# Pooling after the product by banded matrices, GpSimd freed of products in the front, 44 transposed expert tiles prepared ahead on GpSimd's queue

## The chip, the cores and the metric

One core of a Trainium2 chip runs the whole program in one launch. The metric is the device time of one execution, in microseconds (us). Engines are named as in the profile: PE is TensorE, DVE is VectorE, ACT is ScalarE, POOL is GpSimd, SP is SyncE, which issues most of the DMAs.

## The reference, cut to what matters

The input is 512 tokens of 1024 numbers. Two blocks follow each other. The first one is a pooling mixer: `h = x @ w_in`, whose first 2048 columns are `u` (four groups of 512) and the others `z`. For group g with window w in (2, 4, 8, 16):

```python
csum = jnp.cumsum(u, axis=1)
lag = jnp.pad(c, ((0, 0), (w, 0), (0, 0)))[:, :S]
cnt = jnp.minimum(t + 1, w)
outs.append((c - lag) / cnt - u[:, :, g])     # mean of the last w tokens, less the token
m = einsum('bsgc,gcd->bsgd', m, w_grp) * scale
return (m * jax.nn.silu(z)) @ w_out           # then layer_norm(alpha * x + y)
```

The second block computes six modulation vectors `ada = silu(c) @ w_ada + b_ada`, then a gated convolution and a linear recurrence on `h @ w_in`, a head-wise norm and `@ w_out`. After a second norm comes a product-key expert layer: each token chooses 16 of 16384 experts in each of 8 heads, and each chosen expert adds `gate * gelu(h . U[e]) * V[e]`. A last norm ends the program.

## The kernel before, in words

All large products are made in split precision. A weight tile `wraw` is loaded by SP (`wload`, line 124), ACT rounds it to `whi` (L113), and DVE (L117) or POOL (L115) subtracts to get the rest `wlo`. `mm3` (L139 to L141) then makes three PE products for one: high by high, high by low, low by high. A counter, `nload`, deals the subtractions out between DVE and POOL, with the constant `NZ` and the line `nload[1] = 3` setting how many POOL gets.

**The front** (0 to about 355 us in the profile) handles the four pooling groups. `z_group` makes the gate columns, `x_group` makes the windowed sums of x itself on DVE (doubling steps `sw`, L240, then `xe`, L244 to L247, and its split `al`), before any product. It works from `xT`, which POOL builds by four additions at L210. `m_group` multiplies the pooled input with w_in, `gate_group` with w_grp, `y_group` with w_out. The last group, `last_group`, does the latter two in halves. Beside them run the modulation vectors: `ada` loads pieces of w_ada (`araw`) and adds them up on DVE (`acc`, L341, L343), and `ada_fin` splits one sum (`ahl`: ACT, then POOL), reduces it over the partitions by two PE products (L352, L353), adds the bias (L354) and stores 512 numbers to `ada_d` (L355). The table `AF_` says where in a group's turn the four `ada_fin` of the group before are called. The pieces `ahl` share four buffers with `araw`.

**The middle** (371 to about 700 us) has the convolution and recurrence in chunks, the product with w_out, the second norm, the queries and the scores. In this stretch `pre_u` turns 20 tiles of U (128 experts each) round ahead of time: for each half tile four loads `praw` of 64 KB (L535), one DVE transpose to `put` (L540), and a store to the DRAM tile `ut_d`. All loads and stores go through SP's queue.

**The gate tables** (700 to 955 us) are made by one-hot products (L1133, L1135, L1136), and beside them the first expert tiles are worked on by `stage_a`, which makes `U tile @ h`. Here U tiles come in three ways, by tile number i: below `NU` a load of the prepared `ut` from `ut_d`; from there up to tile 37 a load of the raw rows turned by PE (L882, with ACT L884 and DVE L886 behind it); in the last loop a raw load `uraw` and a DVE transpose of the whole tile (L540).

**The last loop** (about 1055 to 1900 us) works through the other expert tiles: `stage_a`, the gates, and the product with V. Beside it POOL issues 256 indirect DMAs (L1181, `gu` and `gv`) for one block of tokens, whose products DVE makes (L1193, L1204).

A scheduler orders the instructions of each engine ahead of time from estimated costs; on the chip each engine and each queue then runs its own list strictly in order, waiting on semaphores.

Of the kernel before, what the change touches and what calls it, by code (L numbers as in the profile page):

```python
# [7 lines left out]
F32 = mybir.dt.float32  # L8
# [36 lines left out]
GP0 = 4  # L45
GL = 1
GE = 117
NU = 20
PU = (1,)
CB = 13  # L50
PL = 0
# [6 lines left out]
UB = 2  # L58
NQ = 3
LAG = 1  # L60
NUR = 3
NP = (0, 1)
HP = ()
WQ = 1
# [15 lines left out]
def _body(tc, nc, a, outer):  # L80
# [51 lines left out]
    def wcols(w, c0, n):  # L132
        return wload(w[:, c0:c0 + n].rearrange("(k p) c -> p k c", p=P), KD)
# [39 lines left out]
    sp_ = p1.enter_context(tc.tile_pool(name="sp_", bufs=3))  # L173
    adp = p1.enter_context(tc.tile_pool(name="adp", bufs=1))
    xT = xp.tile([P, KD, T], F32, name="xT")

    def act_tiles():
        return ([act.tile([P, 2, T], F32R, name="ah", tag="ah") for _ in range(4)],
# [2 lines left out]
    def at(pair, k):  # L181
        return pair[0][k // 2][:, k % 2, :], pair[1][k // 2][:, k % 2, :]
# [32 lines left out]
    def cv(name, i=0, n=1):  # L215
        return cols[:, col[name][0] + i:col[name][0] + i + n]

    def z_group(g, other=()):
        r = []
        for c in range(4):  # L220
            next(iter(other), None)
            if b_first:
                b = b_first.pop(0)
            else:
                w = wcols(w_in, 2048 + (g * 4 + c) * P, P)
                b = bank()
                for k in range(KD):
                    mm3(b, (w[0][:, k], w[1][:, k]), at(xhl, k), k == 0, k == KD - 1)
            r.append(sm.tile([P, T], F32, name="sz", tag="sz", bufs=5))
            S.activation(r[c], b, AF.Silu)  # L230
        return r

    def x_group(g, xg):
        w_ = WINDOWS[g]
        for q in range(4):
            src = xT[:, 2 * q:2 * q + 2, :]
            cur, step = src, 1
            while step < w_:
                nxt = sp_.tile([P, 2, T], F32, name="sw", tag="sw")
                V.tensor_tensor(nxt[:, :, step:], cur[:, :, step:], cur[:, :, :T - step], op=OP.add)  # L240
                S.activation(nxt[:, :, :step], cur[:, :, :step], AF.Copy)
                cur, step = nxt, 2 * step
            e = sp_.tile([P, 2, T], F32, name="xe", tag="sw")
            V.scalar_tensor_tensor(e, cur, 1.0 / w_, src, op0=OP.mult, op1=OP.subtract)  # L244
            n = w_ - 1
            V.tensor_tensor(e[:, :, :n], cur[:, :, :n], rcnt[:, None, :n].to_broadcast([P, 2, n]), op=OP.mult)
            V.tensor_tensor(e[:, :, :n], e[:, :, :n], src[:, :, :n], op=OP.subtract)  # L247
            split(xg[0][q], xg[1][q], e)
            yield

    def m_group(g, xg):
        r = []
        for c in range(4):
            w = wcols(w_in, g * 512 + c * P, P)
            b = bank()
            for k in range(KD):
                mm3(b, (w[0][:, k], w[1][:, k]), at(xg, k), k == 0, k == KD - 1)
            h = sm.tile([P, T], F32R, name="sh", tag="sh")
            l = sm.tile([P, T], F32R, name="sl", tag="sl")
            split(h, l, b)  # L260
            r.append((h, l))
        return r

# [108 lines left out]
    b = bank()  # L372
# [155 lines left out]
    U, W = a["expert_u_2"][0], a["expert_v_2"][0]  # L528
    ut_d = tc.dram_tile([max(1, NU), P, 2, KD * 64], F32, name="ut_d")
    npre = 0  # L530

    def u_load(raw, i, a0, na):

        for q in (0, 2, 1, 3):
            nc.sync.dma_start(raw[32 * q:32 * q + 32],  # L535
                              U[i * P + a0 * 32:i * P + (a0 + na) * 32, q * 256:(q + 1) * 256].rearrange("(a r) d -> r a d", r=32))

    def u_turn(ut, raw):

        V.transpose(out=ut.rearrange("p k (a r) -> p a k r", r=32), in_=raw.rearrange("p a (c k) -> p a k c", k=KD))  # L540

    def pre_u(n):

        nonlocal npre
        for _ in range(n):
            if npre < NU:
                for h in range(2):
                    raw = up.tile([P, 2, 256], F32, name="praw", tag="praw")
                    u_load(raw, npre, 2 * h, 2)
                    ut = up.tile([P, KD, 64], F32, name="put", tag="put")  # L550
                    u_turn(ut, raw)
                    nc.sync.dma_start(ut_d[npre, :, h], ut.rearrange("p k e -> p (k e)"))
                npre += 1
# [664 lines left out]
    urp = outer.enter_context(tc.tile_pool(name="urp", bufs=NUR, reuse_waits="tile"))  # L1218
# [77 lines left out]
```

## Time and profile before

| | |
|---|---|
| median of 3 runs | 1996.67 us (1991.03 to 1996.69) |
| profiled execution | 1993.15 us, its span 1991.4 us |
| mean granted PE clock | 0.968 of full speed |
| busy share of the span | PE 90%, DVE 90%, ACT 42%, POOL 37% |
| chain that ended last | DVE 36%, DMA 24%, PE 17%, issue 12%, ACT 7% |

Between the profiled execution's time and its span lie 1.75 us. The busy shares are means over stages with different limits, so the views by stretch of time say more than this table: in one stretch PE may be full and DVE loose, in the next the other way round.

### The profile page before, as it was taken

To read this page: it belongs to the slowest core of one execution; us is meant where nothing else is said; L and a number is where in the kernel's file an instruction comes from. 1 tells how busy PE (TensorE), PEld (TensorE's weight loads), DVE (VectorE), ACT (ScalarE), POOL (GpSimd) and SP (SyncE) were. 2 spreads that over 40 slices of the span, in tenths; PEclk is the share of its full clock that TensorE was granted. 3 is DMA by queue.
4 is the path that set the end of the run, shared out by engine and by line. 5 is a ranking of instruction groups with operands and counts; after the bars stand their busy time and mean duration, and the time that the engine had idled before them with its cause. 6 is when DMAs were issued, how large, how long until landed. Compare 5 with 4: busy or idle time off the path is not lost.

```text
span 1991.4 us, 26565 instructions
## 1 busy us (share of the span) xinstructions
PE 1800.5 (90%) x9003; PEld 1568.3 (79%) x9003; DVE 1783.6 (90%) x3088; ACT 830.8 (42%) x1318; POOL 727.5 (37%) x492
## 2 busy tenths in 40 slices
PE   8999889896899978888887999998999998989997
PEld 6787677765689978888766898888888887878886
DVE  8989888889868999996897998999999999999956
ACT  4433333444553339988332332333232333332334
POOL 3113222333351000000133655556565556565514
PEclk9999999998899989999998999999999999999999
DMA  5554574465554233545959999999999999999922
GB/s 163 180 166 128 190 250 131 140 203 179 172 159 135 76 112 139 202 179 205 294 199 281 299 285 292 302 296 309 306 298 296 310 299 289 305 293 306 293 102 96
DMA packets 288293, 441.13 MB, mean 222 GB/s; under 512 B 24600, under 2 KB 203652, under 8 KB 285084
## 3 DMA queue, kind: packets, MB, share of 16 engines
q1 hardware_dynamic: 251292, 305.19, 51.1%
q0 software_dynamic: 36864, 134.23, 20.5%
q8 instruction: 71, 1.16, 0.2%
q14 instruction: 66, 0.54, 0.1%
HBM read 393.11 MB, written 46.23 MB: 221 GB/s over the span
## 4 chain that ended last, share of the span: by engine, by line
DVE 36%; DMA 24%; PE 17%; issue 12%; ACT 7%; SPq 2%; POOL 2%; DVEq 0%; POOLq 0%; ACTq 0%
DMA uraw<-in_expert_u 11%; DVE ut L540 5%; DMA gu<-in_expert_u,idx 3%; DMA gv<-in_expert_v,idx 3%; DMA araw<-in_w_ada 3%; PE bank L139 3%; PE bank L141 3%; PE bank L140 3%; ACT gs L1136 2%; DVE acc L1204 2%; DVE ul L117 2%; DVE wlo L117 2%; ACT o L1098 2%; DVE junk L1193 2%; DVE sw L240 2%
## 5 line engine op out<-in xcount | busy, mean ns | idle before, releaser
L115 POOL TENSOR_TENSOR wlo<-wraw,whi 128x1024 fp32r<-128x1024 f32 x111 | 292.3, 2635 | 782.4 <-ACT whi L113 766.8
L141 PE MATMUL aux<-h2h,ul 128*128 128x384 f32 x1024 | 360.7, 353 | 59.8 <-DVE ul L117 53.5
L139 PE MATMUL aux<-h2h,uh 128*128 128x384 f32 x1024 | 355.9, 348 | 4.9 <-ACT uh L884 1.8
L140 PE MATMUL aux<-h2l,uh 128*128 128x384 f32 x1024 | 353.6, 345 | 0.0
L113 ACT ACTIVATE whi<-wraw 128x1024 fp32r<-128x1024 f32 x218 | 228.3, 1051 | 196.4 <-DMA wraw<-in_expert_v 68.5
L140 PE MATMUL o<-wlo,wh 128*128 128x512 f32 x756 | 297.7, 394 | 13.8 <-DVE wlo L117 13.7
L141 PE MATMUL o<-whi,wl 128*128 128x512 f32 x756 | 296.6, 392 | 0.0
L139 PE MATMUL o<-whi,wh 128*128 128x512 f32 x756 | 290.1, 395 | 5.2 <-ACT whi L113 5.2
L141 PEld LDWEIGHTS aux<-h2h,ul 128*128 128x128 f32 x1024 | 198.6, 194 | 76.6 <-DVE ul L117 68.7
L1181 POOL DMA_INDIRECT gv<-in_expert_v,idx x128 | 186.8, 1460 | 186.0 <-DVE acc L1204 150.4
L1181 POOL DMA_INDIRECT gu<-in_expert_u,idx x128 | 167.5, 1309 | 161.3 <-DVE junk L1193 127.7
L139 PEld LDWEIGHTS aux<-h2h,uh 128*128 128x128 f32 x1024 | 198.6, 194 | 10.3 <-ACT gl L905 2.4
L113 ACT ACTIVATE uh<-ut 128x1024 fp32r<-128x1024 f32 x90 | 95.3, 1058 | 262.2 <-PE aux L140 174.5
L540 DVE STREAM_TRANSPOSE ut<-uraw 128x1024 f32<-128x1024 f32 x90 | 200.0, 2222 | 4.7 <-DMA uraw<-in_expert_u 4.7
L140 PEld LDWEIGHTS aux<-h2l,uh 128*128 128x128 f32 x1024 | 197.9, 193 | 3.7
L1193 DVE SCALAR_TENSOR_TENSOR junk<-gu,hrow 128x1024 bf16<-128x1024 f32 x128 | 168.3, 1315 | 19.8 <-DMA gu<-in_expert_u,idx 19.6
L1204 DVE SCALAR_TENSOR_TENSOR acc<-gv,cf,acc 128x1024 f32<-128x1024 f32 x127 | 169.6, 1335 | 17.6 <-DMA gv<-in_expert_v,idx 15.1
L140 PEld LDWEIGHTS o<-wlo,wh 128*128 128x128 f32 x756 | 143.3, 190 | 43.9 <-DVE wlo L117 16.5
L113 ACT ACTIVATE wh<-gl 128x384 fp32r<-128x384 f32 x128 | 66.7, 523 | 253.2 <-PE o L140 234.3
L139 PEld LDWEIGHTS o<-whi,wh 128*128 128x128 f32 x756 | 143.3, 190 | 33.0 <-ACT whi L113 6.1
L141 PEld LDWEIGHTS o<-whi,wl 128*128 128x128 f32 x756 | 143.3, 189 | 30.7
L117 DVE TENSOR_TENSOR wlo<-wraw,whi 128x1024 fp32r<-128x1024 f32 x107 | 150.6, 1409 | 7.2 <-ACT whi L113 7.2
(376 smaller groups left out, 3607.4 us busy)
## 6 DMA issues: line engine op xcount, KB each, us to landing
wraw<-in_expert_v SPq DMA_DIRECT2D x128, 512.0 KB
uraw<-in_expert_u SPq DMA_DIRECT2D x360, 128.0 KB
araw<-in_w_ada SPq DMA_DIRECT2D x96, 256.0 KB
g_d<-gs SPq DMA_DIRECT2D x24, 1024.0 KB
gt<-g_d SPq DMA_DIRECT2D x15, 1536.0 KB
wraw<-in_pool_w_in SPq DMA_DIRECT2D x32, 512.0 KB
wraw<-in_w_in SPq DMA_DIRECT2D x20, 512.0 KB
praw<-in_expert_u SPq DMA_DIRECT2D x160, 64.0 KB
```

Source lines behind the costliest of these rows:

```text
L113: S.activation(hi, src, AF.Copy)
L115: G.tensor_tensor(lo, src, hi.bitcast(F32), op=OP.subtract)
L117: V.tensor_tensor(lo, src, hi.bitcast(F32), op=OP.subtract)
L139: i = PE.matmul(out, lhsT=l[0], rhs=r[0], start=first, stop=False)
L140: PE.matmul(out, lhsT=l[0], rhs=r[1], start=False, stop=False)
L141: PE.matmul(out, lhsT=l[1], rhs=r[0], start=False, stop=last)
L240: V.tensor_tensor(nxt[:, :, step:], cur[:, :, step:], cur[:, :, :T - step], op=OP.add)
L540: V.transpose(out=ut.rearrange("p k (a r) -> p a k r", r=32), in_=raw.rearrange("p a (c k) -> p a k c", k=KD))
L1098: S.activation(o2[:, u], iorow, AF.Abs, bias=sT[:, 1, t0 + u:t0 + u + 1], scale=-1.0)
L1181: G.indirect_dma_start(out=r, out_offset=None, in_=src, in_offset=bass.IndirectOffsetOnAxis(ap=idx[t][:, s:s + 1], axis=0))
L1193: paced(V.scalar_tensor_tensor(junk, r, 1.0, hrow[t], op0=OP.mult, op1=OP.mult, accum_out=cf[t][:, s:s + 1]))
L1204: paced(V.scalar_tensor_tensor(acc[t], r, cf[t][:, s:s + 1], acc[t], op0=OP.mult, op1=OP.add))
```

## The change

1. `u_group` multiplies x with w_in first (x stationary, as many products of 512 columns as `m_group` had), and `pooled` then makes the windowed mean by products with banded 128x144 matrices. In each group these are 32 products of 128 columns and 28 of 16 columns, so 240 in all. `bands` builds the matrices once, with some 40 small DVE instructions. `x_group`, `xT` and the split `al` of the pooled input go; the u columns are split instead (16 ACT, 16 DVE, straight from PSUM). The weights of u come as 2 KB pieces instead of 512 B ones.
2. `NZ` and `nload` leave POOL no product in the front and the middle: POOL's `wlo` go from 111 to 63, DVE's from 107 to 155. The 12 `ahl` go from POOL to DVE.
3. `NU` is 44 instead of 20, and `pre_u` starts in the front: 24 tiles (48 half tiles) there, 20 later. Its loads and stores are issued from POOL's queue (`G`), five DMAs per half tile. In `stage_a` the 18 tiles that PE turned and the first six of the last loop become loads from `ut_d`.
4. `AF_` moves the last four `ada_fin` behind the last `y_group`.

```diff
-AF_ = (1, 1, 0, 0)
-NZ = 1
+AF_ = (1, 1, 1)
+NZ = 1 << 30
-NU = 20
+NU = 44
+NP1 = 1
-    for q in range(4):
-        G.tensor_tensor(xT[:, 2 * q:2 * q + 2, :], xh[:, q].bitcast(F32), xl[:, q].bitcast(F32), op=OP.add)
-    def x_group(g, xg):
...
-    def m_group(g, xg):
...
+    def u_group(g):
+        bs = [bank() for _ in range(NT)]
+        for kk in range(4):
+            w = wload(w_in[kk * 256:(kk + 1) * 256, g * 512:(g + 1) * 512].rearrange("(k p) c -> p k c", p=P), 2)
+            for t in range(NT):
+                s = slice(t * P, (t + 1) * P)
+                for j in range(2):
+                    x = at(xhl, 2 * kk + j)
+                    mm3(bs[t], (x[0][:, s], x[1][:, s]), (w[0][:, j], w[1][:, j]), kk + j == 0, kk == 3 and j == 1)
...
+        for t in range(NT):
+            split(uh[t // 2][:, t % 2], ul[t // 2][:, t % 2], bs[t])
+    def pooled(g, u):
...
+        for c in range(4):
+            b = bank()
+            part = lambda t, i: u[i][t // 2][:, t % 2, c * P:(c + 1) * P]
+            for t in range(NT):
+                m = (band if t else first)[:, :P]
+                o = b[:, t * P:(t + 1) * P]
+                e = o[:, :16]
+                PE.matmul(o, lhsT=part(t, 0), rhs=m, start=True, stop=False)
+                if t == 0:
+                    PE.matmul(e, lhsT=part(t, 0), rhs=rest, start=False, stop=False)
+                else:
+                    PE.matmul(e, lhsT=part(t - 1, 0), rhs=band[:, P:], start=False, stop=False)
+                    PE.matmul(e, lhsT=part(t - 1, 1), rhs=band[:, P:], start=False, stop=False)
+                PE.matmul(o, lhsT=part(t, 1), rhs=m, start=False, stop=True)
...
-        split(hi, lo, acc, True)
+        split(hi, lo, acc)
+                    u_load(raw, npre, 2 * h, 2, G)
...
+                    G.dma_start(ut_d[npre, :, h], ut.rearrange("p k e -> p (k e)"))
-    nload[1] = 3
-    for g in range(4):
-        mhl = m_group(g, xg)
...
+    mhl = pooled(0, u)
+    for g in range(3):
+        pre_u(NP1)
+        u = u_group(g + 1)
+        pre_u(NP1)
+        pre_u(NP1)
         ghl = gate_group(g, mhl, sz)
         if AF_[g] == 1:
             ada_fins()
+        sz = z_group(g + 1)
+        pre_u(NP1)
+        mhl = pooled(g + 1, u)
...
         for _ in y_group(g, ghl):
-            pass
+            pre_u(1)
+    ada_fins()
```

The order of the instructions shows three places, the last of them on two engines. On DVE, at the head of the front (splits of the transposed x, `xl`, then those of the first u weights), the changed program has half-tile transposes between the splits that PE waits for:

```order
L203 TENSOR_TENSOR xl_124<-bank_192,xh_123 128x4x128
L118 TENSOR_TENSOR wlo_242<-wraw_239,whi_241 128x1024
L407 STREAM_TRANSPOSE put_635<-praw_630 128x2x8x32
L203 TENSOR_TENSOR xl_124<-bank_199,xh_123 128x4x128
L407 STREAM_TRANSPOSE put_643<-praw_638 128x2x8x32
L118 TENSOR_TENSOR wlo_272<-wraw_269,whi_271 128x1024
L118 TENSOR_TENSOR wlo_302<-wraw_299,whi_301 128x1024
L407 STREAM_TRANSPOSE put_787<-praw_782 128x2x8x32
L118 TENSOR_TENSOR wlo_332<-wraw_329,whi_331 128x1024
L407 STREAM_TRANSPOSE put_795<-praw_790 128x2x8x32
L118 TENSOR_TENSOR wlo_376<-wraw_373,whi_375 128x1024
```

Before, no transpose stood on DVE ahead of the middle; now each stands in front of a `wlo`, which cannot start until the transpose has its `praw`.

On POOL, in the same place, the list before had the additions to `xT` and the subtractions:

```order
L210 TENSOR_TENSOR xT<-xh,xl 128x1024 x4
L115 TENSOR_TENSOR wlo<-wraw,whi 128x1024 x6
L115 TENSOR_TENSOR ahl<-acc,ahl 128x512
L115 TENSOR_TENSOR wlo<-wraw,whi 128x1024 x2
L115 TENSOR_TENSOR ahl<-acc,ahl 128x512 x3
```

and now has the traffic of the half tiles alone:

```order
L419 DMA ut_d_234<-put_635 128x512
L402 DMA praw_782<-in_expert_u_2 32x2x256 x4
L419 DMA ut_d_234<-put_643 128x512
L402 DMA praw_790<-in_expert_u_2 32x2x256 x4
L419 DMA ut_d_234<-put_787 128x512
```

A store, which waits for its transpose, stands ahead of the four loads of the half tile two further on.

On SP, on the way into `last_group`, whose weights are `pool_w_grp` and the `pool_w_out` behind it, the list before was

```order
L339 DMA araw<-in_w_ada 128x512 x4
L124 DMA wraw<-in_pool_w_grp 128x4x256 x2
L339 DMA araw<-in_w_ada 128x512 x3
L124 DMA wraw<-in_pool_w_in 128x8x128
L339 DMA araw<-in_w_ada 128x512 x2
L124 DMA wraw<-in_pool_w_out 128x2x512 x2
```

and now is

```order
L373 DMA araw<-in_w_ada 128x512 x28
L382 DMA araw<-in_b_ada 1x512 x2
L472 DMA lng<-in_ln_g 128x1024
L472 DMA lnb<-in_ln_b 128x1024
L472 DMA g1r<-ada_d 128x1024
L389 DMA ada_d<-araw 1x512
L382 DMA araw<-in_b_ada 1x512
L389 DMA ada_d<-araw 1x512
L382 DMA araw<-in_b_ada 1x512
L541 DMA acol<-ada_d 128x2x8
L389 DMA ada_d<-araw 1x512 x2
```

followed by loads of `n2` and of `vin2` (the latter from `ada_d`) and only then by the two loads of `pool_w_grp`. So these weights stand behind the four stores that end the `ada_fin`. On PE the same place reads now

```order
L141 MATMUL bank_3076<-wlo_2983,sh_2530 128x512
L142 MATMUL bank_3076<-whi_2982,sl_2531 128x512
L386 MATMUL aux_3108<-ahl_3109,ones_88 1x512
L387 MATMUL aux_3108<-ahl_3110,ones_88 1x512
L386 MATMUL aux_3119<-ahl_3120,ones_88 1x512
L387 MATMUL aux_3119<-ahl_3121,ones_88 1x512
L386 MATMUL aux_3130<-ahl_3131,ones_88 1x512
L387 MATMUL aux_3130<-ahl_3132,ones_88 1x512
L386 MATMUL aux_3141<-ahl_3142,ones_88 1x512
L387 MATMUL aux_3141<-ahl_3143,ones_88 1x512
L571 MATMUL aux_3416<-ident_84,vin2_3174 128x128
L140 MATMUL bank_3236<-sh_2742,whi_3194 128x256
```

with the last product of `y_group` (bank_3076) and the first of `last_group` (bank_3236) on either side of all four `ada_fin` and of a transpose that reads `vin2`, loaded from `ada_d`. Before, the `ada_fin` pairs stood between products of `m_group` and `last_group`.

## Rows read from the trace of the kernel before

**Rows 1.** The page: busy time of the engines; the chain that ended last.

```profile
PE 1800.5 (90%) x9003; PEld 1568.3 (79%) x9003; DVE 1783.6 (90%) x3088; ACT 830.8 (42%) x1318; POOL 727.5 (37%) x492
...
DVE 36%; DMA 24%; PE 17%; issue 12%; ACT 7%; SPq 2%; POOL 2%; DVEq 0%; POOLq 0%; ACTq 0%
```

**Rows 2.** Busy us by stretch, front: PE, PEld, DVE, ACT, POOL, clock, DMA, GB/s.

```profile
100.00:150.00 50.00, 50.00 (x217) 40.32 (x216) 44.97 (x61) 15.42 (x24) 9.04 (x4) 1.00 0.53 162
...
sum 350.00, PE 324.36 PEld 260.99 DVE 315.66 ACT 128.25 POOL 94.06; mean PE 46.34 PEld 37.28 DVE 45.09 ACT 18.32 POOL 13.44
```

**Rows 3.** Groups by line, 0 to 350 us: operation, count, busy us, mean ns, idle, releasers.

```profile
L343 DVE SCALAR_TENSOR_TENSOR acc<-araw,cact,acc 128x512 f32<-128x512 f32 x84 | 70.8, 844 | 14.4 <-DMA araw<-in_w_ada 13.3 <-DVE acc L343 0.3
...
L117 DVE TENSOR_TENSOR wlo<-wraw,whi 128x1024 fp32r<-128x1024 f32 x39 | 55.7, 1430 | 1.9 <-ACT whi L113 1.9
L115 POOL TENSOR_TENSOR wlo<-wraw,whi 128x1024 fp32r<-128x1024 f32 x19 | 54.9, 2892 | 178.9 <-ACT whi L113 178.8
...
L240 DVE TENSOR_TENSOR sw<-xT 128x1022 f32<-128x1022 f32 x16 | 23.8, 1487 | 0.0
...
L117 DVE TENSOR_TENSOR al<-xe,ah 128x1024 fp32r<-128x1024 f32 x16 | 22.7, 1423 | 0.4 <-ACT ah L113 0.4
...
L117 DVE TENSOR_TENSOR sl<-bank,sh 128x512 fp32r<-128x512 f32 x16 | 10.8, 681 | 4.3 <-ACT sh L113 4.3
```

**Rows 4.** Groups by line, 700 to 955 us, the gate tables.

```profile
L1135 PE MATMUL bank<-og,o 128*128 128x128 f32 x768 | 99.6, 283 | 20.5 <-ACT gs L1136 10.5 <-ACT o L1099 9.8 <-DVE og L1133 0.2
...
L1136 ACT ACTIVATE gs<-bank 128x512 f32<-128x512 f32 x96 | 93.7, 1088 | 0.4 <-DMA g_d<-gs 0.3
...
L882 PE MATMUL aux<-ident,uraw 128*128 128x128 f32 x144 | 21.5, 276 | 2.9 <-ACT gl L905 2.9
L884 ACT ACTIVATE uh<-aux 128x512 fp32r<-128x512 f32 x35 | 20.8, 611 | 5.1 <-PE aux L882 5.1
```

**Rows 5.** Tile ahl, 310 to 345 us: ns min/median/max, first and last start us.

```profile
L113 ACT ACTIVATE ahl<-acc x4: 622/632/632, 316.3 to 329.4; 128x512 fp32r<-128x512 f32 x4
L115 POOL TENSOR_TENSOR ahl<-acc,ahl x4: 1287/1786/2060, 317.7 to 330.7; 128x512 fp32r<-128x512 f32 x4
...
L352 PE MATMUL aux<-ahl,ones x4: 393/396/397, 318.0 to 334.3; 128*1 128x512 f32 x4
```

**Rows 6.** Groups by line, 371 to 600 us, the middle.

```profile
L115 POOL TENSOR_TENSOR wlo<-wraw,whi 128x1024 fp32r<-128x1024 f32 x27 | 67.3, 2494 | 121.2 <-ACT whi L113 109.3 <-DMA praw<-in_expert_u 11.9
...
L540 DVE STREAM_TRANSPOSE put<-praw 128x512 f32<-128x512 f32 x40 | 46.2, 1158 | 12.8 <-DMA praw<-in_expert_u 12.7
...
L620 PE MATMUL aux<-sq,blk 128*128 128x512 f32 x16 | 13.2, 932 | 27.4 <-ACT sq L616 27.4
```

**Rows 7.** Busy us by stretch, the last loop.

```profile
1100.00:1900.00 800.00, 746.33 (x3626) 667.37 (x3625) 760.86 (x767) 254.06 (x356) 458.65 (x291) 0.98 1.01 298
```

**Rows 8.** Groups by line, 1100 to 1900 us, the last loop.

```profile
L540 DVE STREAM_TRANSPOSE ut<-uraw 128x1024 f32<-128x1024 f32 x85 | 189.3, 2227 | 0.0
L1181 POOL DMA_INDIRECT gv<-in_expert_v,idx x128 | 186.8, 1460 | 186.0 <-DVE acc L1204 150.4 <-DMA uraw<-in_expert_u 12.4 <-issue 6.4
...
L1181 POOL DMA_INDIRECT gu<-in_expert_u,idx x119 | 157.7, 1325 | 139.9 <-DVE junk L1193 112.6 <-DMA uraw<-in_expert_u 9.2 <-issue 8.1
...
L113 ACT ACTIVATE uh<-ut 128x1024 fp32r<-128x1024 f32 x86 | 91.0, 1058 | 241.8 <-PE aux L140 174.5 <-DVE ut L540 42.4 <-issue 17.0
```

**Rows 9.** The chain, 1050 to 1085 us: start us, us, what.

```profile
1056.72 11.19 DMA uraw<-in_expert_u
```

**Rows 10.** Line 1181, all of the run: ns min/median/max.

```profile
L1181 POOL DMA_INDIRECT gv<-in_expert_v,idx x128: 939/1296/3298, 1123.3 to 1881.7; - x128
```

**Rows 11.** POOL's timeline, 1450 to 1458 us: start us, us, what.

```profile
1453.13 3.30 POOL L1181 DMA_INDIRECT gv<-in_expert_v,idx  x1 [2.81 <-DVE acc L1204]
```

**Rows 12.** DVE's timeline beside it.

```profile
1453.26 1.21 DVE L117 TENSOR_TENSOR wlo<-wraw,whi 128x1024 fp32r<-128x1024 f32 x1
1454.39 1.21 DVE L1193 SCALAR_TENSOR_TENSOR junk<-gu,hrow 128x1024 bf16<-128x1024 f32 x1
```

More of the change, by code (lines that the diff above doesn't have):

```diff
@@ L60 @@
 LAG = 1
-NUR = 3
+BW = P + 16
 NP = (0, 1)
@@ L172, in _body @@
     sm = front2.enter_context(tc.tile_pool(name="sm", bufs=8, side="right"))
-    sp_ = p1.enter_context(tc.tile_pool(name="sp_", bufs=3))
+    up = p1.enter_context(tc.tile_pool(name="up1", bufs=2))
     adp = p1.enter_context(tc.tile_pool(name="adp", bufs=1))
-    xT = xp.tile([P, KD, T], F32, name="xT")
     def act_tiles():
@@ L216, in cv, with z_group @@
         return cols[:, col[name][0] + i:col[name][0] + i + n]
-    def z_group(g, other=()):
+    def z_group(g):
         r = []
         for c in range(4):
-            next(iter(other), None)
             if b_first:
@@ L231, in z_group @@
         return r
-    def x_group(g, xg):
[L234 to L244, printed above, removed]
-            n = w_ - 1
[L246 to L249, printed above, removed]
@@ L251, in m_group, with bands @@
-    def m_group(g, xg):
+    def bands():
+        wide = xp.tile([P, BW], F32, name="wide")
+        past = xp.tile([P, BW], F32, name="past")
+        G.iota(wide, pattern=[[1, BW]], base=0, channel_multiplier=-1, allow_small_or_imprecise_dtypes=True)
+        V.tensor_scalar(past, wide, 0.0, None, op0=OP.is_ge)
+        for g, w_ in enumerate(WINDOWS):
+            n = w_ - 1
+            f = xp.tile([P, BW], F32, name="bandf", tag="bandf", bufs=2)
+            V.scalar_tensor_tensor(f, wide, float(w_), past, op0=OP.is_lt, op1=OP.mult)
+            V.scalar_tensor_tensor(f[:, :P], ident, -float(w_), f[:, :P], op0=OP.mult, op1=OP.add)
+            band = xp.tile([P, BW], F32R, name=f"band{g}")
+            V.tensor_copy(band, f)
+            e = xp.tile([P, 16], F32, name="edge", tag="edge", bufs=2)[:, :n]
+            V.scalar_tensor_tensor(e, rcnt[:, :n], float(w_), past[:, :n], op0=OP.mult, op1=OP.mult)
+            V.scalar_tensor_tensor(e, ident[:, :n], -float(w_), e, op0=OP.mult, op1=OP.add)
+            first = xp.tile([P, BW], F32R, name=f"first{g}")
+            V.tensor_copy(first, f)
+            V.tensor_copy(first[:, :n], e)
+            rest = xp.tile([P, 16], F32R, name=f"rest{g}")
+            V.tensor_scalar(rest, ident[:, :16], 0.0, None, op0=OP.mult)
+            V.tensor_tensor(rest[:, :n], e, first[:, :n].bitcast(F32), op=OP.subtract)
+            band_.append((band, first, rest))
@@ new lines, in _body @@
+    band_ = []
+    def u_group(g):
[7 more added lines that the diff above has]
+                    mm3(bs[t], (x[0][:, s], x[1][:, s]), (w[0][:, j], w[1][:, j]), kk + j == 0, kk == 3 and j == 1)
+        uh = [act.tile([P, 2, T], F32R, name="ah", tag="ah") for _ in range(2)]
+        ul = [act.tile([P, 2, T], F32R, name="al", tag="al") for _ in range(2)]
+        for t in range(NT):
+            split(uh[t // 2][:, t % 2], ul[t // 2][:, t % 2], bs[t])
+        return uh, ul
@@ L252, in m_group @@
+    def pooled(g, u):
         r = []
+        band, first, rest = band_[g]
         for c in range(4):
-            w = wcols(w_in, g * 512 + c * P, P)
             b = bank()
-            for k in range(KD):
-                mm3(b, (w[0][:, k], w[1][:, k]), at(xg, k), k == 0, k == KD - 1)
+            part = lambda t, i: u[i][t // 2][:, t % 2, c * P:(c + 1) * P]
[10 more added lines that the diff above has]
+                PE.matmul(o, lhsT=part(t, 1), rhs=m, start=False, stop=True)
@@ L258, in m_group @@
             h = sm.tile([P, T], F32R, name="sh", tag="sh")
             l = sm.tile([P, T], F32R, name="sl", tag="sl")
-            split(h, l, b)
+            S.activation(h, b, AF.Copy, scale=1.0 / WINDOWS[g])
+            V.scalar_tensor_tensor(l, b, 1.0 / WINDOWS[g], h.bitcast(F32), op0=OP.mult, op1=OP.subtract)
             r.append((h, l))
@@ L359, in ada_fins, with u_load, u_turn, pre_u @@
             ada_fin(j, accs.pop(j))
+    U, W = a["expert_u_2"][0], a["expert_v_2"][0]
+    ut_d = tc.dram_tile([max(1, NU), P, 2, KD * 64], F32, name="ut_d")
+    npre = 0
+    def u_load(raw, i, a0, na, q_=nc.sync):
+        for q in (0, 2, 1, 3):
+            q_.dma_start(raw[32 * q:32 * q + 32],
+                              U[i * P + a0 * 32:i * P + (a0 + na) * 32, q * 256:(q + 1) * 256].rearrange("(a r) d -> r a d", r=32))
+    def u_turn(ut, raw):
+        V.transpose(out=ut.rearrange("p k (a r) -> p a k r", r=32), in_=raw.rearrange("p a (c k) -> p a k c", k=KD))
+    def pre_u(n):
+        nonlocal npre
+        for _ in range(n):
+            if npre < NU:
+                for h in range(2):
+                    raw = up.tile([P, 2, 256], F32, name="praw", tag="praw")
+                    u_load(raw, npre, 2 * h, 2, G)
+                    ut = up.tile([P, KD, 64], F32, name="put", tag="put")
+                    u_turn(ut, raw)
+                    G.dma_start(ut_d[npre, :, h], ut.rearrange("p k e -> p (k e)"))
+                npre += 1
+    u = u_group(0)
     sz = z_group(0)
+    bands()
     vin = pers.tile([P, P], F32, name="vin")
@@ L390, in _body @@
             ada_fins()
-        xg = act_tiles()
-        sz = z_group(g + 1, x_group(g + 1, xg))
+        sz = z_group(g + 1)
+        pre_u(NP1)
+        mhl = pooled(g + 1, u)
         if AF_[g] == 2:
@@ L527, in _body @@
     up = p2.enter_context(tc.tile_pool(name="up", bufs=2, reuse_waits="tile"))
[L528 to L553, printed above, removed]
     lam = cv("lru_lambda_2", 0, 4)
@@ L1217, in _body @@
     banks(outer, AUX)
-    urp = outer.enter_context(tc.tile_pool(name="urp", bufs=NUR, reuse_waits="tile"))
+    urp = outer.enter_context(tc.tile_pool(name="urp", bufs=3, reuse_waits="tile"))
     for i in range(P):
```

6 lines of the change are left out of this document (removed).

## The prediction

> **What bounds the kernel now.** I read the page first [rows 1]: PE and DVE are both busy for 90% of the span, and the chain that ended last spends 36% on DVE, 24% on DMA and only 17% on PE. The mean hides stages with different limits, so the views by stretch come next, then the groups by line within a stretch. The sum is made against the profiled execution, 1993.15 us, which lies 3.5 us below the median of 1996.67.
>
> In the front PE is nearly full: 50.00 us of 50 in one stretch, 324.36 of 350 over all [rows 2]. The same row has DVE busy for 315.66. So PE leads, DVE follows a step behind, and at most 350 - 324.36 = 25.6 us of waiting can be won there. DVE's busy time is inflated: the split `wlo` takes 1430 ns on the mean [rows 3], and 1.21 us where POOL computes nothing beside it [rows 12]. In the middle, PE's large wait is at L620, the head norm, 27.4 us, and it waits there for ACT, whose input comes from DVE [rows 6]. In the gate tables PE stands behind ACT: 10.5 and 9.8 us of its idle time end with ACT instructions [rows 4]. In the last loop DVE is busy 760.86 us of 800 and the DMA engines are full (1.01, 298 GB/s) [rows 7].
>
> **The change part by part.**
>
> *Small products on PE, front.* `u_group` does the work that `m_group` did. New are 128 products of 128 columns and 112 of 16. The trace has no banded product of this type. The nearest row is L1135: 768 products of 128 columns with as many weight loads are busy for 99.6 us, 0.130 us each [rows 4]. 128 x 0.130 = 16.6. The 16 columns cost between nothing and the same 0.130; half of it gives 112 x 0.065 = 7.3. Together **+24**. Lower end: a quarter of a 512-column product (50.00 / 217 = 0.230 us [rows 2]) for the first kind, nothing for the second, 128 x 0.058 = +7. Upper end: each as dear as a 512-column one, 240 x 0.230 = +55. PE is full there, so all of it lies on the path.
>
> *DVE in the front.* Gone are 40 window sums at about 1.49 us (59), the 16 `al` (22.7) [rows 3] and the 16 `xe` of the same size, as much again, 105 in all, and small edge pieces. New are 48 half-tile transposes at 1158 ns (55.6) [rows 6], POOL's 19 `wlo` [rows 3] at 1.21 (23), 28 splits of 512 columns at 681 ns (19), 98 in all, and some 40 small ones for the bands. So the work is equal. What falls is the holding: 39 x (1.43 - 1.21) = 8.6 us on `wlo` alone, and the same on other splits. PE waits less; between nothing and all 25.6. I take **-18**, nearer the upper end, since the two-input DVE instructions show the holding in most of their rows.
>
> *The last four `ada_fin`.* They ran beside other products. Now PE meets all four, then a transpose that reads their result, and `last_group`'s weights stand behind their stores on SP, as the order shows. Before, the first product of the four and the last lie 334.3 - 318.0 = 16.3 us apart, 5.4 each [rows 5]: the pieces share four buffers, so one waits for the store of another. With DVE's 681 ns in place of POOL's 1786 the step is 4.3, four steps 17. Waiting behind them: the weight load, its rounding and split, some 4 us as an estimate from 512 KB at 298 GB/s [rows 7] and 1.2 for DVE. `y_group`'s last adds overlap the first step. **+16**, from 0 (all four end beside `y_group`) to +24.
>
> *The middle.* 27 `wlo` go from POOL (2494 ns) [rows 6] to DVE, 27 x 1.21 = 33 us more there; the DVE instructions that POOL's held up get back about as much. The transposes stay 40. SP loses 200 DMAs that stood ahead of weight loads. **-5**, from -27 (the whole wait at L620) to +24 (POOL too slow, below).
>
> *The gate tables.* 18 tiles give up 36 ACT instructions of 611 ns [rows 4] for 18 of 1058 [rows 8]: 22 - 19 = **-3**. PE's 144 transposes (21.5 us) [rows 4] go too, but lie beside ACT, which had 0.4 us idle before L1136. From -21 to 0.
>
> *The last loop.* Six tiles lose their DVE transpose: 6 x 2.227 [rows 8] = 13.4. Part of the opening wait for raw tiles, 11.19 us in one piece [rows 9], may go with it, since the prepared tiles need no turning; part may stay, since the DMA engines are full. **-14**, from -25 (both) to -2.
>
> *POOL's queue.* 240 DMAs in the front, 200 in the middle. At the shortest issue, 939 ns [rows 10], that is 226 and 188 us, less than the stretches they lie in (about 320 and 229), so **0**. At the mean it is more: first rival.
>
> Sum: 24 - 18 + 16 - 5 - 3 - 14 = 0, so **1993**. Its own range is 1975 to 2012.
>
> **The rivals.**
>
> *POOL's issues are too slow (slower).* The program has no plain DMA on POOL's queue; the nearest rows are the indirect ones. Their mean in the last loop is (186.8 + 157.7) / 247 = 1.39 us [rows 8]. One took 3.30 us while DVE ran two two-input instructions back to back beside it, and ended only after them [rows 11, 12]. The front has runs of such instructions (84 `acc` [rows 3], the `wlo`). At 1.39 the 240 issues take 334 us against 320, the 200 of the middle 278 against 229. Two buffers only let POOL run two half tiles ahead, and on DVE each transpose stands before a `wlo` that PE needs, so DVE waits, then PE. It decides from 1.33 us an issue in the front, 1.15 in the middle. Price: the 18 us of relief are not won, and +20 in the middle: 1993 + 18 + 20 = 2031. Against it: while DVE waits, nothing holds POOL up, and a plain DMA need not read an index tile. The Trainium skill ("SBUF — State Buffer", section "SBUF: two separate sides") says that a DVE instruction with two SBUF inputs locks out only a GpSimd operation that itself reads SBUF. By that rule plain loads would not be held, and this rival would fall; the 3.30 us agree only in so far as an indirect DMA counts as such a reader. The same section warns that DVE's two-port modes starve descriptors written by GpSimd; no run here shows that for a plain DMA.
>
> *The holding was worth more (faster).* If the small products cost their lower end (+7), all 25.6 us of PE's wait go, the `ada_fin` cost +6 because DVE reaches them earlier, and the middle gains 8: 7 - 26 + 6 - 8 - 3 - 14 = -38, 1955. For it: DVE is late nearly everywhere before L620 and PE follows it. Against: DVE's total work hardly falls.
>
> *The prepared tiles do not shorten the last loop.* A prepared tile has as many bytes as a raw one, and if the full DMA engines set the pace [rows 7], the DVE time saved is idle time: -2 instead of -14, 2005.
>
> **How the numbers follow.** A measurement can tell about 0.3% from no change here, 6 us: 1990.7 to 2002.7 is "same". Forecast 0.36, POOL too slow 0.26, holding worth more 0.26, last loop unmoved 0.12. The forecast's range splits as 0.14 faster, 0.13 same, 0.09 slower; POOL's rival is slower but for 0.01; the second is faster but for 0.01; the last gives 0.03 faster, 0.03 same, 0.06 slower. Together 0.42 faster, 0.18 same, 0.40 slower. The range must hold the middles of both large rivals: 1948 to 2034.
>
> **What would show it.** PE busy in the front should rise by some 24 us, and its count by 240. The mean of `wlo` on DVE should fall to 1.21 us in the first 600 us. A gap of PE between `y_group` and `last_group` of 16 us, ended by the load of `pool_w_grp` or the transpose of `vin2`, would bear out the third term. DVE idle time ended by `praw` loads in the front of more than 20 us would bear out the first rival, and so would POOL issues above 1.3 us. The last loop should be 14 us shorter from its first gather to the end. What would make the prediction wrong outright: 128-column products at the price of 512-column ones, or a POOL issue of 2 us and more.

## The result, and the profile after

The changed kernel takes 2056.14 us (median; 2051.07 to 2068.56), the kernel before 1993.85 in the same comparison: a ratio of 1.0326, 95% interval 1.0286 to 1.0366. It is 3.3% slower. The forecast was 1993 with a range up to 2034, so it was wrong, by more than the range allowed. Each view below comes from one profiled execution of a kernel.

The page of the changed kernel, its busy times and its chain, answers to [rows 1]:

```profile
span 2052.4 us, 27048 instructions
...
PE 1831.3 (89%) x9099; PEld 1598.4 (78%) x9099; DVE 1730.8 (84%) x3121; ACT 819.0 (40%) x1260; POOL 804.0 (39%) x869
```

DVE got 53 us less to do (1783.6 before), PE 31 more, and the span grew by 61.0. To see where, I cut both spans at the same five instructions. Views by line give their first and last starts. The kernel before (last add of the front, products with g1, one-hot gates, first gather):

```profile
L309 DVE TENSOR_TENSOR ya<-ya,bank x8: 666/683/689, 332.2 to 368.6; 128x512 f32<-128x512 f32 x8
...
L737 DVE TENSOR_TENSOR ot<-bank,g1r x8: 678/687/692, 558.6 to 584.6; 128x512 f32<-128x512 f32 x8
...
L1133 DVE TENSOR_SCALAR og<-iorow,sT x384: 293/337/349, 745.1 to 939.1; 128x128 f32<-128x128 f32 x192
...
L1181 POOL DMA_INDIRECT gu<-in_expert_u,idx x128: 941/1064/4492, 1055.3 to 1828.5; - x128
```

The changed kernel, in the same order, and the last gather, which answers to [rows 10]:

```profile
L343 DVE TENSOR_TENSOR ya<-ya,bank x8: 671/681/689, 383.2 to 415.7; 128x512 f32<-128x512 f32 x8
...
L772 DVE TENSOR_TENSOR ot<-bank,g1r x8: 648/682/692, 601.5 to 624.3; 128x512 f32<-128x512 f32 x8
...
L1168 DVE TENSOR_SCALAR og<-iorow,sT x384: 295/352/2512, 824.2 to 1024.3; 128x128 f32<-128x128 f32 x192
...
L1216 POOL DMA_INDIRECT gu<-in_expert_u,idx x128: 939/1302/1988, 1139.3 to 1887.0; - x128
L1216 POOL DMA_INDIRECT gv<-in_expert_v,idx x128: 939/1298/3293, 1200.5 to 1937.4; - x128
```

| stretch, ended by | before, us | after, us | difference |
|---|---|---|---|
| front, last `ya` add | 368.6 | 415.7 | +47.1 |
| middle, last `ot` | 216.0 | 208.6 | -7.4 |
| second norm, queries, scores, first `og` | 160.5 | 199.9 | +39.4 |
| gate tables, first `gu` | 310.2 | 315.1 | +4.9 |
| last loop, last `gv` | 826.4 | 798.1 | -28.3 |
| rest of the span | 109.7 | 115.0 | +5.3 |

The two large rows are the front and the second norm. Differences of some 5 us say little: over the changed kernel and its variants below, the gate tables take 310 to 315 us.

**The front.** The sum row of the stretches from 0 to 350 us answers to [rows 2]:

```profile
sum 350.00, PE 331.31 PEld 274.90 DVE 249.78 ACT 101.82 POOL 132.48; mean PE 47.33 PEld 39.27 DVE 35.68 ACT 14.55 POOL 18.93
```

DVE fell from 315.66 to 249.78 and PE did not gain by it. I took each product's distance to the next one's start: up to the distance at full clock it is work; the rest is a delay if it is at most 1.25 times as much again, and a gap if it is longer. So PE's 416 us divide, from its first product on, into some 321 of the old products, 24 of banded ones, 25 of delays and 42.5 of gaps; before, 369 us into 322, 0, 12.7 and 30.7. The difference is about 24 + 12 + 12. The delays are only in part a lower clock: the records have the clock at 0.50 for 10.2 us of the front before and for 61.4 after, and 30.7 of these 61.4 lie within and right behind the four rows of banded products. Windows of 5 us of PE show it (columns: window, its length, PE busy and count, granted clock, DMA share, GB/s):

```profile
60.00:65.00 5.00, 5.00 (x41) 0.99 0.61 206
65.00:70.00 5.00, 5.00 (x25) 0.50 0.77 260
70.00:75.00 5.00, 5.00 (x15) 0.50 0.62 191
75.00:80.00 5.00, 5.00 (x23) 0.98 0.91 272
```

PE is busy throughout. The banded products of group 0 run from 61.3 to 70.9; the granted clock falls to 1.2 GHz (0.50) among them, and the 512-column products behind them still run at it: 15 in 5 us in place of 23. Their starts are 0.427 us apart there and 0.227 at full clock, so the 30.7 us cost some 14, as an estimate.

DVE's groups in the same 350 us answer to [rows 3]:

```profile
L377 DVE SCALAR_TENSOR_TENSOR acc<-araw,cact,acc 128x512 f32<-128x512 f32 x84 | 62.5, 747 | 16.4 <-DMA araw<-in_w_ada 15.8
L118 DVE TENSOR_TENSOR wlo<-wraw,whi 128x1024 fp32r<-128x1024 f32 x50 | 60.8, 1216 | 36.5 <-ACT whi L114 36.4
L407 DVE STREAM_TRANSPOSE put<-praw 128x512 f32<-128x512 f32 x48 | 55.7, 1160 | 14.1 <-DMA praw<-in_expert_u 14.1
```

The holding is gone (1216 ns, 1430 before), and DVE now waits for others. POOL's new DMAs, by line, for all of the run:

```profile
L402 POOL DMA_DIRECT2D praw<-in_expert_u x352: 533/533/800, 1.5 to 644.4; - x176
...
L419 POOL DMA_DIRECT2D ut_d<-put x88: 557/586/966, 21.6 to 648.4; - x88
```

An issue takes 0.53 us, and the longest 0.97: five take 2.7 us, where the slow rival needed 6.7 (320 us for 48 half tiles). 68 of them lie wholly within an `acc` or a `wlo` of DVE, which read two inputs, and took 0.53 to 0.60 us.

**The second norm.** PE's longest single wait of the whole run, 27.1 us, is here. The waits from 623 to 655 us, then POOL's and DVE's timelines at its end:

```profile
PE aux L523 <- DVE xn L510: 27.1, 1, 27.1
POOL ut_d L419 <- DVE put L407: 18.8, 3, 13.2
ACT whi L114 <- DMA wraw<-in_w_q: 11.2, 3, 6.3
...
ACT xn L507 <- DMA ut_d<-put: 3.4, 1, 3.4
```

```profile
642.20 0.59 POOL L419 DMA_DIRECT2D ut_d<-put  x1 [13.21 <-DVE put L407]
642.78 2.12 POOL L402 DMA_DIRECT2D praw<-in_expert_u  x4
...
648.43 0.56 POOL L419 DMA_DIRECT2D ut_d<-put  x1 [2.95 <-DVE put L407]
...
650.27 0.49 POOL L498 TENSOR_SCALAR rr<-rq,rs 128x1 f32<-128x1 f32 x2
```

```profile
647.03 1.09 DVE L407 STREAM_TRANSPOSE put<-praw 128x512 f32<-128x512 f32 x1 [2.01 <-DMA praw<-in_expert_u]
650.57 1.42 DVE L510 TENSOR_SCALAR xn<-ya,rr 128x1024 f32<-128x1024 f32 x2 [2.44 <-POOL rr L498]
```

The last half tiles stand in DVE's and POOL's lists ahead of the norm's `xn` and `rr`. DVE reaches those transposes only behind splits of w_q, and these wait for ACT's roundings, which wait 11.2 us for their loads. ACT's first `xn` stands behind the same roundings, and its second one waits 3.4 us for a `ut_d` store. So tiles that are wanted some 400 us later (the last prepared tile is loaded back at 1062 us) hold up the norm. The kernel before began `xn` on ACT 9.9 us after the first `ot` (568.5 and 558.6), the changed one 42.2 us after it (643.7 and 601.5), when all the products with w_out were over.

### The profile page after: what moved, and what is told of

It is laid out like the page before. It is cut to its first block, busy times and chain, and to the rows that moved or that the text cites. A ratio compares the mean times of both kernels' runs of the same rounds, so it can differ in the third digit from the quotient of the medians.

```text
span 2052.4 us, 27048 instructions
## 1 busy us (share of the span) xinstructions
PE 1831.3 (89%) x9099; PEld 1598.4 (78%) x9099; DVE 1730.8 (84%) x3121; ACT 819.0 (40%) x1260; POOL 804.0 (39%) x869
## 4 chain that ended last, share of the span: by engine, by line
DVE 23%; DMA 17%; PE 11%; issue 9%; ACT 5%; POOL 3%; SPq 1%; DVEq 0%; POOLq 0%; ACTq 0%
DMA uraw<-in_expert_u 8%; DVE ut L407 5%; DMA gu<-in_expert_u,idx 4%; DMA wraw<-in_expert_v 2%; DMA gv<-in_expert_v,idx 2%; DVE og L1168 2%; DVE acc L1239 2%; DVE junk L1228 2%; PE aux L142 2%; DVE ul L118 2%; PE aux L141 2%; PE aux L140 2%; ACT gs L1171 1%; ACT o L1133 1%; DVE wl L118 1%
## 5 line engine op out<-in xcount | busy, mean ns | idle before, releaser
L116 POOL TENSOR_TENSOR wlo<-wraw,whi 128x1024 fp32r<-128x1024 f32 x63 | 166.0, 2635 | 479.7 <-ACT whi L114 452.2
L118 DVE TENSOR_TENSOR wlo<-wraw,whi 128x1024 fp32r<-128x1024 f32 x155 | 189.7, 1224 | 74.9 <-ACT whi L114 74.0
L1216 POOL DMA_INDIRECT gv<-in_expert_v,idx x128 | 182.6, 1427 | 166.6 <-DVE acc L1239 106.4
L402 POOL DMA_DIRECT2D praw<-in_expert_u x352 | 187.1, 538 | 9.2 <-issue 5.9
L407 DVE STREAM_TRANSPOSE ut<-uraw 128x1024 f32<-128x1024 f32 x84 | 188.3, 2242 | 0.1
L1239 DVE SCALAR_TENSOR_TENSOR acc<-gv,cf,acc 128x1024 f32<-128x1024 f32 x127 | 176.0, 1386 | 9.9 <-DMA gv<-in_expert_v,idx 9.5
L114 ACT ACTIVATE uh<-ut 128x1024 fp32r<-128x1024 f32 x84 | 88.9, 1059 | 223.2 <-PE aux L141 144.9
```

Source lines behind the costliest of these rows:

```text
L402: q_.dma_start(raw[32 * q:32 * q + 32], U[i * P + a0 * 32:i * P + (a0 + na) * 32, q * 256:(q + 1) * 256].rearrange("(a r) d -> r a d", r=32))
L1216: G.indirect_dma_start(out=r, out_offset=None, in_=src, in_offset=bass.IndirectOffsetOnAxis(ap=idx[t][:, s:s + 1], axis=0))
L1239: paced(V.scalar_tensor_tensor(acc[t], r, cf[t][:, s:s + 1], acc[t], op0=OP.mult, op1=OP.add))
```

## The experiments

Twelve kernels ran. Ratios are to the kernel before, with 95% intervals.

**e1_sp_queue.** The half tiles' DMAs on SP's queue.

```diff
-                    u_load(raw, npre, 2 * h, 2, G)
+                    u_load(raw, npre, 2 * h, 2)
...
-                    G.dma_start(ut_d[npre, :, h], ...)
+                    nc.sync.dma_start(ut_d[npre, :, h], ...)
```

> The changed kernel with the loads and stores of the half tiles issued from SP's queue again, all else as changed. Theory one: the 27 us gap of PE ahead of the second norm comes from the late half tiles, whose place in the lists follows from their being on GpSimd's queue; then the gap goes and the time falls by 20 to 35 us against the changed kernel. Theory two: the gap comes from the number of tiles (44), whatever the queue; then it stays and the time is within 8 us, or longer, because SP's queue now has 200 DMAs more in the front.

2058.4 us, 1.0322 (1.0269 to 1.0375): no change in the time, but two large ones within it. The transposes and the first `xn`:

```profile
L407 DVE STREAM_TRANSPOSE put<-praw x88: 1082/1153/1231, 22.4 to 591.5; 128x512 f32<-128x512 f32 x88
...
L507 ACT ACTIVATE xn<-ya x4: 1046/1060/1062, 645.6 to 666.2; 128x1024 f32<-128x1024 f32 x4
```

The last transpose is at 591.5 in place of 647, `xn` begins 8 us after the first `ot` (637.5), and no gap stands before it. The stretch behind the middle takes 166.4 us, 33 less. The front takes 32 more (its last add at 447.6), and PE's gaps there grow from 42.5 to 67. Half tiles and weights now come late by the same queue. Up to 350 us, DVE's transposes and ACT's roundings wait so:

```profile
DVE put L407 <- DMA praw<-in_expert_u: 69.2, 27, 5.9
```

```profile
ACT whi L114 <- DMA wraw<-in_pool_w_in: 33.1, 8, 6.7
```

In the changed kernel these waits are 14.1 and 15.4 us. Theory one was right on the gap and missed what POOL's queue is worth in the front; theory two had the front's loss in view.

**e2_nu40.** `NU = 40`.

> The changed kernel with 40 instead of 44 prepared tiles, so that none is left over behind the middle's loop. Theory one (the place of the last half tiles follows from the queue, not from their number): the gap ahead of the second norm shrinks by less than half, the time by less than 12 us. Theory two (too many tiles): the gap goes, and the time falls by 20 us or more.

2019.09 us, 1.0123 (1.0082 to 1.0165), 37 us under the changed kernel. `xn` begins 8 us after the first `ot`. This is what theory two expected; with e1 both the queue and the number matter. The stretch of the second norm takes 163.7 us, 36 less. That the whole gains as much is in part chance: the last loop gives 16 back (814.3), since only two of its first six tiles are prepared, and the end of the span is 14 shorter (101.0), which no run explains.

**f3_early44.** 44 tiles, 28 of them in the front, none left behind the middle's loop.

```diff
-        pre_u(NP1)
+        pre_u(2)
         u = u_group(g + 1)
...
-        pre_u(NP1)
+        pre_u(2 if g == 0 else 1)
         mhl = pooled(g + 1, u)
```

> The changed kernel with 44 tiles, but 28 instead of 24 in the front, so that none is left behind the middle's loop. Theory one: the gap of 27 us comes from the last four tiles' place (they hold memory and GpSimd's list until the second norm); it goes, and the time is 25 to 40 us under the changed kernel's. Theory two: it is the number 44 itself; then the gap stays.

2025.72 us, 1.0134 (1.0092 to 1.0176), 30 under the changed kernel, as theory one has it. `xn` begins 8 us after the first `ot` again, and the stretch of the second norm takes 37 us less (162.8). It is not the number 44.

**h1_nu20.** `NU = 20`, `NP1 = 0`, no tile in the front.

> The changed kernel with 20 prepared tiles, all in the middle as before the change, still on GpSimd's queue (16 in the loop, four behind it). Theory one: the gap ahead of the second norm comes from the four tiles behind the loop on GpSimd's queue, whatever the total; it stays at 15 us or more. Theory two: it comes from the total of 44; it goes. The front tells what the 24 early tiles cost there: if their DMAs make PE's weights late, it ends 5 to 12 us earlier than the changed kernel's; if they are hidden, within 3 us. The last loop should be 24 to 29 us longer, since it turns its first six tiles itself again.

2063.65 us, 1.0328 (1.0289 to 1.0368). PE's waits from 607 to 645 us:

```profile
PE aux L523 <- DVE xn L510: 31.7, 1, 31.7
```

The gap is there with 20 tiles. So it is the four tiles that `pre_u(NU)` leaves behind the middle's loop, if their traffic is on POOL's queue. On SP's queue (before, and e1) the lists have them earlier. The front ends 9 us earlier than the changed kernel's (407.2 to 416.4): by the third group PE's gaps are 9 us there, 21 in the changed kernel, so the 24 early tiles cost PE some 9 to 12 us. Late weights are one part of it. ACT's first rounding, in the changed kernel and then here:

```profile
13.02 1.06 ACT L114 ACTIVATE whi<-wraw 128x1024 fp32r<-128x1024 f32 x1 [4.21 <-DMA wraw<-in_pool_w_in]
```

```profile
10.21 1.06 ACT L114 ACTIVATE whi<-wraw 128x1024 fp32r<-128x1024 f32 x1 [1.27 <-DMA wraw<-in_pool_w_in]
```

The changed kernel's other two large gaps there (3.7 us at 245.5, 2.9 at 340.1) end with a `wlo` whose weights were on the chip and rounded: DVE comes to it late. For the first of them, its rounding and DVE's list:

```profile
244.26 1.06 ACT L114 ACTIVATE whi<-wraw 128x1024 fp32r<-128x1024 f32 x1 [5.21 <-PE bank L142]
```

```profile
243.82 0.49 DVE L375 TENSOR_SCALAR acc<-araw,cact 128x512 f32<-128x512 f32 x1 [1.60 <-DMA araw<-in_w_ada]
...
246.27 1.08 DVE L407 STREAM_TRANSPOSE put<-praw 128x512 f32<-128x512 f32 x1
247.28 0.71 DVE L377 SCALAR_TENSOR_TENSOR acc<-araw,cact,acc 128x512 f32<-128x512 f32 x1
247.91 1.22 DVE L118 TENSOR_TENSOR wlo<-wraw,whi 128x1024 fp32r<-128x1024 f32 x1
```

h1 takes out the early transposes together with their loads, and has neither gap; no run parts the two. From the first to the last gather it takes 823 us, 25 more, as expected.

**e3_no_bands.** 32 products of 512 columns in place of the 240 banded ones.

```diff
-            for t in range(NT):
...
-                PE.matmul(o, lhsT=part(t, 1), rhs=m, start=False, stop=True)
+            PE.matmul(b, lhsT=part(0, 0), rhs=at(xhl, 0)[0], start=True, stop=False)
+            PE.matmul(b, lhsT=part(3, 1), rhs=at(xhl, 1)[0], start=False, stop=True)
```

> The changed kernel with the 240 banded products left out: in their place stand 32 products of 512 columns (two for each output tile), so the windowed mean is not computed. Theory one: the front is bound by PE, the banded products cost 24 us at full clock and about 12 more through the lower granted clock that follows them; then the front ends 27 to 33 us earlier (36 less 7.4 for the products put in) and the granted clock of the front is 0.98 or more. Theory two: PE waits for DVE or loads anyway and the products fill gaps; then the front ends less than 12 us earlier.

2032.63 us, 1.0191 (1.0151 to 1.023). The third `y_group` ends 29.3 us earlier (320.3 to 349.6), and PE to 320 us is at full clock:

```profile
0.00:320.00 320.00, 297.90 (x1305) 0.99 0.79 242
```

The end of the front comes only 16 us earlier, since PE then reaches the last `ada_fin` before DVE does:

```profile
PE aux L377 <- ACT ahl L114: 17.7, 3, 16.2
```

Theory one held as far as the third group. For the front as a whole it did not: it expected 27 to 33 us, and had not in view what the sums behind the third group give back.

**e4_fins.** The sums six each in the first two groups' turns.

```diff
-        for j in range(4 * g, 4 * g + 4):
+        for j in range(6 * g, min(6 * g + 6, 12)):
             accs[j] = ada(j)
```

(with six buffers for `acc`)

> The changed kernel with the twelve modulation sums made six each in the first two groups' turns, so that no ada_fin stands between the last y_group and last_group. Theory one: the gap of PE there (16 us from its first ada_fin to the first product of last_group) goes, at no cost elsewhere, since DVE has idle time in the front; the front ends 10 to 16 us earlier. Theory two: last_group's own weight loads set the gap; then it ends less than 5 us earlier.

2037.99 us, 1.0227 (1.0187 to 1.0268), 18 us under the changed kernel. The last add of the front is at 399.8, 15.9 earlier, and the gap is gone. This is theory one.

**f1_fins_nu40.** e2 and e4 together.

> The changed kernel with both edits that gained: 40 tiles instead of 44, and the modulation sums six each in the first two groups. If the two losses are separate, the gains add: 37 and 18 us, to about 2001. If they share the same slack (the middle catches up what the front loses), the sum is under 40 us, 2016 or more.

2014.79 us, 1.0104 (1.0068 to 1.0141). The median is 4 us under e2's, the profiled span 12 (2005.2 to 2017.0; f1's profiled execution is the fastest of its four), where 18 were hoped for. The front's 16 us are there (401.5 to 417.6); the gains do not add in full.

**f2_mix.** On f1: the banded products of groups 1 to 3 stand between z_group's chunks.

```diff
-        sz = z_group(g + 1)
+        mhl = []
+        sz = z_group(g + 1, pooled(g + 1, u, mhl))
...
-        mhl = pooled(g + 1, u)
```

> The run before (40 tiles, sums early) with the banded products of groups 1 to 3 written chunk by chunk between the chunks of z_group's 512-column products. Theory one: PE's granted clock falls because the banded products stand in a row; spread out, the slow stretches behind them shrink, and the front gets 5 to 9 us shorter. Theory two: the clock falls whenever such products run, in a row or not; no change within 3 us.

2009.63 us, 1.0064 (1.004 to 1.0088). Its interval and f1's overlap, so the time tells nothing. The clock does: windows of 10 us at the banded products of group 2, f1 first, then f2 (there they stand in four bunches of 15 from 195 to 220 us, two of them in the first window):

```profile
220.00:230.00 10.00, 10.00 (x52) 9.52 (x52) 6.20 (x10) 2.41 (x5) 3.71 (x7) 0.59 0.73 220
```

```profile
210.00:220.00 10.00, 10.00 (x61) 8.50 (x59) 6.37 (x9) 4.92 (x8) 5.42 (x10) 1.00 0.56 171
220.00:230.00 10.00, 10.00 (x45) 7.93 (x44) 8.13 (x11) 2.06 (x3) 2.73 (x5) 1.00 0.79 249
```

Of the twelve bunches only one, with an idle time of PE of 4.5 us within it, has the clock at 0.50; the whole row of group 0, which f2 leaves as it was, has it for 10.2 us as before. The second `y_group` ends 10 us earlier (251.9 to 261.9), but the new order then puts `ada_fin` waits into the last group (that of 4.5 us among them), and the front ends 4 us later. So theory one holds for the clock, and its 5 to 9 us for the front did not come.

**f4_no_gpsimd.** The kernel before, with POOL's products of the front and middle on DVE.

```diff
-NZ = 1
+NZ = 1 << 30
...
-        split(hi, lo, acc, True)
+        split(hi, lo, acc)
...
-    nload[1] = 3
+    nload[1] = 1 << 30
```

> The kernel before with GpSimd's products in the front and the middle given to DVE (the splits of weights and of the modulation sums), nothing else. Theory one: DVE's held instructions cost PE little, since PE waited only some 11 us for DVE in the front; then the time is within 10 us of before, and DVE's busy time in the front changes by less than its 19 added splits. Theory two: the holding was on the path; then 15 us or more faster.

1980.94 us, 0.994 (0.9912 to 0.9969): 13 us faster, between the two theories. The profiled execution, 1992.32, is the slowest of its ten, so its stretches do not show those 13 us. DVE's busy time in the front falls (315.66 before) although 31 splits come to it:

```profile
sum 350.00, PE 324.05 PEld 261.96 DVE 307.10 ACT 128.99 POOL 16.23; mean PE 324.05 PEld 261.96 DVE 307.10 ACT 128.99 POOL 16.23
```

The third `y_group` ends 19 us earlier (284.4 to 303.5), 13 of it gaps (21 to 8); `last_group` and the first norm then give 16 back, the largest wait of PE there being

```profile
PE aux L461 <- DVE rw L427: 7.0, 1, 7.0
```

**g1_fins, g2_prep, g3_both.** On f4: the sums earlier; the six tiles 38 to 43 prepared in place of 14 to 19; both.

```diff
+PREP = tuple(range(14)) + tuple(range(38, 44))
...
-        ty = 4 if i < NU else ATY if i < RT else 2
+        ty = 4 if i in PREP else ATY if i < RT else 2
```

> The kernel before without GpSimd's products in the front and middle (the run of that name), and with the modulation sums one step earlier, so that none of their ends stands near last_group. If the gaps ahead of last_group and of the first norm there (5 to 7 us each in that run) come from those ends, 8 to 15 us less than that run's 1981, about 1970; if they come from the norm's own chain, within 5 us of it.

> The kernel before without GpSimd's products in the front and middle, and with the 20 prepared tiles chosen otherwise: the first 14, and the six that the last loop begins with (38 to 43), in place of 14 to 19, which PE turns. Theory one: what the changed kernel won behind the scores (24 us) came from these six tiles alone; then the last loop gets 15 to 29 us shorter, the gate tables 2 to 6 us longer, and the time falls by 10 to 25 us to 1956 to 1971. Theory two: it came from the many prepared tiles in the gate tables; then no gain.

> Both edits on the kernel before without GpSimd's products in the front and middle. If they are independent the gains add: about 1945 to 1965.

g1: 1982.06 us, 0.9949 (0.9927 to 0.9971), no gain on f4. Its trace has the same wait of the norm as f4's,

```profile
PE aux L466 <- DVE rw L432: 7.0, 1, 7.0
```

so that wait does not come from the sums' ends, and the second case of the expectation holds (the norm's own chain). g2: 1970.84 us, 0.9901 (0.9871 to 0.9931). The last loop of f4, then of g2:

```profile
1052.00:1879.00 827.00, 764.11 (x3678) 678.98 (x3676) 781.30 (x786) 260.80 (x365) 460.56 (x302) 0.97 1.02 298
```

```profile
1055.00:1858.00 803.00, 749.86 (x3617) 667.62 (x3616) 763.13 (x775) 256.19 (x359) 463.03 (x301) 0.97 1.02 302
```

The loop takes 23 to 24 us less, with the same number of prepared tiles as before the change. So the six that it begins with give it, as theory one says. The gate tables take 5.9 more (306.7 to 312.6), and of the whole time 10 us are won, by the medians (1980.94 to 1970.84). g3: 1971.87 us, 0.991 (0.9886 to 0.9935), the same as g2 and not the 1945 to 1965 expected, since g1 adds nothing. g2 is faster than both kernels of this study.

## Why the prediction was wrong, step by step

- **Small products, +24.** Right as a price at full clock: 24 by the distances above, 27 by whole blocks of 15, which start 1.7 us apart before the clock falls. The clock was missing. Each of the four rows takes PE to 1.2 GHz for part of the row and for the products behind it: some 12 to 14 us more (e3, f2).
- **DVE in the front, -18.** This step failed: of PE's 25.6 us of waiting it took 18 to go with DVE freed. Part of them was the start and the `ada_fin`. f4 shows what freeing DVE is worth up to the third group, 13 us of gaps and 4 of short delays; in the changed kernel the gaps there are 21 as before. By h1 the early tiles take that gain away again. Where it goes is shown in part: 3 us to late weights at the start, 6.5 to two `wlo` that DVE reaches late, one of them with a transpose ahead of it. The sum had the loads' issue on POOL, and neither their place among the transfers (DMA share 0.80, 0.82 and 0.74 in the first three stretches of 50 us, 0.54, 0.58 and 0.53 before) nor what the transposes' place ahead of a `wlo`, which the order showed, costs PE. (The 40 window sums were 57.4 us, not 59, which changes nothing.)
- **The last `ada_fin`, +16.** About right: the gaps of the last stage go from 9.6 to 21.8, 12 more, and e4 wins 16 by moving them.
- **The middle, -5.** Right: -7.4.
- **POOL's queue, 0.** This is the step that failed by most. I weighed how long the issues take and found them hidden, which they are. I did not ask what stands behind them. The second norm has no term at all; it lost 39 us, and 33 to 37 of them go when the four tiles in front of it are moved or left out (33.5 in e1, 36 in e2, 37 in f3), while with only 20 tiles it stays if four of them are there (h1). The instructions could be read in the order of the changed kernel: the last transposes stood directly ahead of `xn`.
- **The gate tables, -3, and the last loop, -14.** Together -17, measured -23.4: +4.9 and -28.3. The six tiles are worth more than the DVE time of their transposes, 13.4, and most of it comes in the opening of the loop: in g2, 16 of the 23 us are won by the 41st of the 256 gathers. The gate tables' +4.9 stays open; h1, with 20 prepared tiles, has the same 315.1 us, so it is not the 44.
- **The end, no term.** +5.3 us, not tried. In the other runs this stretch takes 101 to 118 us.
- **The rivals.** POOL too slow: refuted, 0.53 us an issue against a threshold of 1.15. The rule of the Trainium skill ("SBUF — State Buffer", "SBUF: two separate sides"), that a two-input DVE instruction locks out only a GpSimd operation that reads SBUF, fits these plain loads and stores, none of which took over 0.97 us. The other two rivals did not come either: the last loop did get shorter, and the holding did go, but what it gave PE was taken away. The range lost the result because every slow case hung on that one rival.

By stretch, as measured in the two profiles, 47 - 7 + 39 + 5 - 28 + 5 = 61; forecast were 22, -5, 0, -3, -14 and 0.

## What to carry to other kernels

When work is moved to another queue, read the order for what stands behind its last piece, and not only how long the pieces take; four tiles wanted much later cost 33 to 37 us here, while the time of the issues stayed hidden. A cheap row of narrow products can cost PE its clock beyond the row, and in f2 spreading it between wide ones kept the clock up. Prepare ahead what the next stage needs first: six tiles at the head of the last loop made it 23 to 24 us shorter, and the whole run 10, with no tile more than before.

## What the runs showed of the hardware that was not expected

PE's granted clock fell to 0.50 while PE was busy without a break, in all four rows of 60 products with 128 and 16 columns, which started 0.08 to 0.15 us apart at full clock; with 15 of them at a time between 512-column products it stayed at 1.00 in eleven cases of twelve, and in the twelfth PE had been idle for 4.5 us. A plain DMA issued by POOL took 533 ns (64 KB, landing 3.3 us later), and not over 600 in the 68 cases that lay within a two-input instruction of DVE; the indirect ones took up to 4.5 us beside such instructions.
